# A hybrid decoder step on one core: warm-up products over ones, unscaled value sums, squares added on VectorE, and another order of the output chunks

## The chip, the cores and the metric

The kernel runs as one program on one core of a Trainium2 chip. The metric is the device time of one execution in microseconds (us); lower is better. The engines are PE (matrix products; PEld is its weight load), DVE (VectorE), ACT (ScalarE), POOL (GpSimd) and SP, whose queue issues nearly all transfers.

## The reference, cut to what matters

Two layers are applied to a prompt of 512 tokens and to 32 sample tokens (8 sequences of 4) with a page cache of 2,048 positions. All values are float32.

```python
def _layer(x, ...):
    h = _rmsnorm(x, norm_w)
    z = h @ w_in                                     # 1024 -> 3584 columns
    rq, rk, rv, rg, mq, mk, mv, mg, pu, pg = split(z)
    r_o, S_new = _retention(rope(rq), rope(rk) / 8, rv, S0, gn_w)
    m_o = moba_attend(rope(rmsnorm(mq)), rope(rmsnorm(mk)), mv)
    p_o, buf_new = _pool_mixer(pu, pool_buf, ...)
    mix = concat(r_o * silu(rg), m_o * silu(mg), p_o * silu(pg))
    return x + mix @ w_out, S_new, mk, mv, buf_new   # x twice: prompt, sample
```

The RMS norm is `x * rsqrt(mean(x*x) + eps) * norm_w`. Since a token's `rsqrt` is one number, a projection may be taken of `x * norm_w` and scaled by it afterwards; layer 0 of the kernel does that.

## The kernel before, in words

**Products.** Each dense product is split in two parts per operand: `whl` holds a weight slice's high part (a rounded copy by ACT) and its low part (the difference, by DVE or POOL), `XT` the same of the tokens, features on partitions. A product is three passes (`PASSES`, L475): high by high, low tokens by high weights, high tokens by low weights. The weights come in chunks of four slices of 256 features each: `mv`, `mq`, `mk`, `pu`, `pg`, `mg`, `rq`, `rv`, `rk`, `rg`, then the output projection `o0`, `o1` (384 columns) and `o2` (256 columns). A token tile (128 tokens) of a 384-column chunk is 24 products of 128x384, of `o2` 24 of 128x256.

**Order.** `_Plan` (L119) lays out all engines ahead of time while the program is built: each task asks for an engine (`R`), names flags that it needs and buffers that it takes, and the earliest task by planned times is written next. Each engine then runs its instructions in that fixed order and waits only on semaphores. Dense products have the lowest rank and fill the gaps; attention over cached pages (`dec`, `pv`), transposes (`tr`) and prompt attention (`att`) go ahead of them. Five `whl` buffers hold one chunk's four slices and the next chunk's first. A changed duration, rank or flag can move instructions everywhere.

**Start.** `start` (L1640) loads the first tokens on ACT's queue; `load_weights` and `load_tokens` take the rest in turn on SP's. Tokens lie in two halves `h` of 256 and four feature pairs `kp`: `split_tokens` makes `XT` from `mix`, scaled by `ncol` (the norm's weights). `norm_tokens` squares the tokens into `qT` (half 0) and `kT` (half 1), adds over features, and a product with `ones` (`tr<-ones,qT`) sums over partitions. PE's first real work is `mv`, half 0 in the `acc` sums, half 1 in `att`. One product of zeros (`warm`) stands ahead of it.

**Between the layers.** `post_out` adds the residual to a tile of the output projection; with the last chunk the tile is whole and `rmsnorm` of layer 1 can run: ACT squares, POOL takes the root, DVE multiplies, PE transposes (`tr<-cst,qT` for tiles 0 and 1, `kT` for 2 and 3, `PT` for the sample), ACT and DVE write `XT`.

Of the kernel before, what the change touches and what calls it, by code (L numbers as in the profile page):

```python
# [111 lines left out]


SP_PRIO = 2
WARM = 1


class _Plan:
# [198 lines left out]
def trunk(ctx, tc, depth, xp, xt, xs, xst, kv, sret, spool, pt, nrow, ncol, lpar, w384, w256, cst, y0,  # L317
# [108 lines left out]
        G.tensor_tensor(out=out, in0=out, in1=mhalf[:rows, :n], op=OP.pow)  # L426


    order = ["mv", "mq", "mk", "pu", "pg", "mg", "rq", "rv", "rk", "rg", "o0", "o1", "o2"]
    chunks = [(l, n) for l in range(depth) for n in order]  # L430
    wt, raws, readers = {}, {}, {}

# [28 lines left out]
    def split_weights():  # L461
        for ci, (l, n) in enumerate(chunks):
            W2 = 2 * width(n)
            for s_ in slices(n):
                yield R("ACT", [("raw", ci, s_)], ["whl"])
                hl = wt[ci, s_] = buf("whl")
                A.copy(hl[:, 0, :W2], raws[ci, s_][:, :W2])

                def low(hl=hl, W2=W2, ci=ci, s_=s_):
                    yield R("DVE|POOL")  # L470
                    add2(hl[:, 1, :W2], raws[ci, s_][:, :W2], hl[:, 0, :W2].bitcast(F32), OP.subtract)
                    read_raw(ci, s_)
                    X.flag("w", ci, s_)

                X.spawn(low(), 2, X.then())  # L475
# [2 lines left out]
    KS_IN = list(range(8))  # L478
    KS_OUT = [6, 7, 4, 5, 2, 3, 0, 1]

    def tok_piece(ci, n, t, a, ks, i):

        W = width(n)
        k = ks[i]
        w0, w1 = (wt[ci, k // 2][:, lo, (k % 2) * W:(k % 2 + 1) * W] for lo in range(2))
        for j, (xl, wl) in enumerate(PASSES):
            mm(a[:, :W], XT[:, k, xl, t * 128:(t + 1) * 128], w1 if wl else w0,
               start=i == 0 and j == 0, stop=i == 7 and j == 2)

    def feat_piece(ci, n, f, half, a, ks, i):  # L490
# [318 lines left out]
    def layer(l):  # L809
# [702 lines left out]

        def residual():

            for name in ("o0", "o1", "o2"):
# [12 lines left out]
        def post_out(name, t):  # L1528
# [4 lines left out]
            def f(a):  # L1533
                if t < 4:
                    yield R("DVE", got)
                    res = L["res", name, t]
                    out = ytile(t, c0, W)
                    V.tensor_tensor(out=out, in0=col3(a[:, :W]), in1=col3(res[:, :W]), op=OP.add)
                    X.put("acc")
                else:  # L1540
                    yield R("DVE", (), ["t1"])
                    z_ = buf("t1")[:NS, :W]
                    yield from join_sample(a, z_, W)
                    yield R("DVE", got)
                    res = L["res", name, t]
                    V.tensor_tensor(out=z_, in0=z_, in1=res[:NS, :W], op=OP.add)
                X.put("qk")
                if t == 4:
                    yield R("SP")
                    S.dma_start(o_ys[:, c0:c0 + W] if l == depth - 1 else y0[SEQ:, c0:c0 + W], z_)  # L1550
                    at = X.dma(48)
                    X.put("t1", at=at)
                    if name == "o2":
                        X.flag("ys", l + 1, at=at)
                elif l == depth - 1:
                    send(col3(o_yp[t * 128:t * 128 + 128, c0:c0 + W]), out, W / 2)
                elif name == "o2":
                    X.flag("y", l + 1, t)
                    send(col3(y0[t * 128:t * 128 + rows, :]), ytile(t), 512)
            return f  # L1560

        def dense():
# [18 lines left out]
            else:  # L1581

                for h in range(2):
                    for kp in range(4):
                        yield R("PE", [("w", ci, kp), ("xk", h, kp)], [] if kp else ["att" if h else "acc"] * 2)
                        if kp == 0:
                            a = [ps("acc") for _ in range(2)] if h == 0 else [ps("att")] * 2
                            a = a if h == 0 else [x[:, j] for j, x in enumerate(a)]
                        for j in range(2):
                            for k in (2 * kp, 2 * kp + 1):  # L1590
                                tok_piece(ci, "mv", 2 * h + j, a[j], KS_IN, k)
                        if h:
                            X.put("whl")
                    for j in range(2):
# [44 lines left out]

    def start():  # L1640
        yield R("ACT")
        nc.scalar.dma_start(mix[:, 0:2, 0:256], col3_(xt[0, 0]))
        X.use("ACT", 0.06)
        X.flag("xt", 0, 0, at=X.now + 3.0)
        yield R("SP")
        S.dma_start(ncolt, ncol)
        X.flag("ncol", at=X.dma(4))
        X.spawn(load_weights(), 3)
        X.spawn(split_weights(), 4)
        X.spawn(load_tokens(), 2)  # L1650
# [2 lines left out]
        for h in range(2):  # L1653
            for kp in range(4):
                X.spawn(split_tokens(h, kp), 1)
            X.spawn(norm_tokens(h), 2)
        X.spawn(split_sample(), 1)
        layers[0]["begin"]()

# [27 lines left out]
    def split_tokens(h, kp):  # L1687

        cs = slice(256 * h, 256 * h + 256)
        ks = (2 * kp, 2 * kp + 1)  # L1690
        yield R("ACT|DVE", [("xt", h, kp), ("ncol",)])
        for k in ks:
            if X.engine == "ACT":
                A.activation(XT[:, k, 0, cs], mix[:, k, cs], AF.Copy, scale=ncolt[:, k:k + 1])
            else:
                V.tensor_scalar(XT[:, k, 0, cs], mix[:, k, cs], ncolt[:, k:k + 1], None, op0=OP.mult)
        yield R("DVE")
        for k in ks:
            V.scalar_tensor_tensor(XT[:, k, 1, cs], mix[:, k, cs], ncolt[:, k:k + 1], XT[:, k, 0, cs].bitcast(F32),
# [3 lines left out]
    def norm_tokens(h):  # L1703

        cs = slice(256 * h, 256 * h + 256)
        tag = ("qT", "kT")[h]
        for i in range(2):
            yield R("ACT|POOL", [("xt", h, 2 * i), ("xt", h, 2 * i + 1)], [] if i else [tag])
            if i == 0:
                sq = buf(tag)[:, :2048].rearrange("p (k n) -> p k n", k=8)  # L1710
            x = mix[:, 4 * i:4 * i + 4, cs]
            if X.engine == "ACT":
                A.activation(sq[:, 4 * i:4 * i + 4], x, AF.Square)
            else:
                G.tensor_tensor(out=sq[:, 4 * i:4 * i + 4], in0=x, in1=x, op=OP.mult)
        yield R("DVE|POOL")
        add2(sq[:, 0:4], sq[:, 0:4], sq[:, 4:8], OP.add)
        yield R("DVE|POOL")
        add2(sq[:, 0:2], sq[:, 0:2], sq[:, 2:4], OP.add)
        yield R("DVE|POOL")  # L1720
        add2(sq[:, 0], sq[:, 0], sq[:, 1], OP.add)
        yield R("PE", [("zeros",)], ["tr"])
        p = ps("tr")
        for j in range(2):
# [60 lines left out]

    def clear():
        yield R("POOL")
        G.memset(qblk, 0.0)
        G.memset(ones, 1.0)
        X.flag("zeros")  # L1790
        G.memset(mhalf, -0.5)
        for s_ in Sst:
# [3 lines left out]

    def warm(n):

        yield R("PE", [("zeros",)], ["att", "att"])
        o_ = ps("att")[:, 0]  # L1800
        for _ in range(n):
            mm(o_[:, :384], qblk[:, 0, 0:4, :].rearrange("p b r -> p (b r)"),
               qblk[:, 0:2].rearrange("p i b r -> p (i b r)")[:, :384])
        X.put("att", 2)

    layers = [layer(l) for l in range(depth)]
# [3 lines left out]
            yield from layers[l]["dense"]()  # L1810

    X.spawn(start(), 0)
    X.spawn(warm(1), 0)
    X.spawn(clear(), 0)
    X.spawn(dense(), 9)
    X.run()
# [84 lines left out]
```

## Time and profile before

| | us |
|---|---|
| median of 3 runs | 698.95 (697.78 to 700.24) |
| profiled execution | 699.1 |
| its span | 697.3 |
| PE busy | 679.0 (97%) |
| DVE, ACT, POOL busy | 486.5, 334.0, 104.3 |

The profile has one execution. Its span is the time from the first to the last recorded work; the profiled time is 1.8 us longer. A busy PE is not PE at its peak: matmuls are pipelined, and the recorded ends are modelled.

### The profile page before, as it was taken

To read this page: it belongs to the slowest core of one execution; us is meant where nothing else is said; L and a number is where in the kernel's file an instruction comes from. 1 tells how busy PE (TensorE), PEld (TensorE's weight loads), DVE (VectorE), ACT (ScalarE), POOL (GpSimd) and SP (SyncE) were. 2 spreads that over 40 slices of the span, in tenths; PEclk is the share of its full clock that TensorE was granted. 3 is DMA by queue.
4 is the path that set the end of the run, shared out by engine and by line. 5 is a ranking of instruction groups with operands and counts; after the bars stand their busy time and mean duration, and the time that the engine had idled before them with its cause. 6 is when DMAs were issued, how large, how long until landed. Compare 5 with 4: busy or idle time off the path is not lost.

```text
span 697.3 us, 16968 instructions
## 1 busy us (share of the span) xinstructions
PE 679.0 (97%) x5940; PEld 570.0 (82%) x5940; DVE 486.5 (70%) x1155; ACT 334.0 (48%) x847; POOL 104.3 (15%) x132
## 2 busy tenths in 40 slices
PE   7999999999999999999999999999999999999998
PEld 6997767777877887899988778777687878989998
DVE  6889888677663569975494699775846455897642
ACT  7553676652342333364363437676723324256520
POOL 4332223000000012300021223230100000051000
PEclk9999999999999999999999999999999999999999
DMA  9667899699979964335553887999988997020552
GB/s 320 226 214 238 271 317 320 209 293 299 306 246 335 320 243 148 100 127 181 188 174 126 271 256 256 301 320 288 295 281 284 316 308 250 4 96 5 169 181 79
DMA packets 111366, 159.76 MB, mean 229 GB/s; under 512 B 13937, under 2 KB 96114, under 8 KB 111282
## 3 DMA queue, kind: packets, MB, share of 16 engines
q1 hardware_dynamic: 111010, 158.43, 69.8%
q8 instruction: 47, 0.77, 0.4%
q10 hardware_dynamic: 272, 0.26, 0.2%
q14 instruction: 37, 0.30, 0.1%
HBM read 148.80 MB, written 9.84 MB: 228 GB/s over the span
## 4 chain that ended last, share of the span: by engine, by line
PE 79%; DVE 12%; DMA 4%; issue 2%; ACT 2%; POOL 1%; DVEq 0%; ACTq 0%
PE acc L349 50%; PE pv L349 10%; PE dec L349 10%; PE tr L359 5%; PE att L349 4%; DVE whl L311 2%; DMA wraw<-w 2%; DVE qk L311 1%; DVE t L311 1%; DMA pk<-kv 1%; DVE acc L311 1%; DVE qT L311 1%; DMA mix<-xt 1%; DVE P L311 1%; DVE qst L311 1%
## 5 line engine op out<-in xcount | busy, mean ns | idle before, releaser
L349 PE MATMUL acc<-whl,XT 128*128 128x384 f32 (+1 forms) x1680 | 309.9, 337 | 4.1 <-ACT whl L311 3.2
L349 PEld LDWEIGHTS acc<-whl,XT 128*128 128x128 f32 x1680 | 281.3, 189 | 23.5 <-issue 14.5
L349 PE MATMUL acc<-XT,whl 128*128 128x256 f32 (+1 forms) x960 | 136.6, 294 | 0.9 <-ACT pt L311 0.5
L349 PEld LDWEIGHTS acc<-XT,whl 128*128 128x128 f32 x960 | 124.0, 189 | 9.6 <-issue 6.4
L311 ACT CAST whl<-wraw 128x768 fp32r<-128x768 f32 (+1 forms) x100 | 76.8, 782 | 47.2 <-PE acc L349 37.7
L311 DVE TENSOR_TENSOR whl<-wraw,whl 128x768 fp32r<-128x768 f32 (+1 forms) x92 | 85.4, 941 | 18.1 <-ACT whl L311 17.0
L349 PE MATMUL dec<-pk,qblk 128*32 128x256 f32 x768 | 49.5, 383 | 0.7 <-issue 0.6
L349 PEld LDWEIGHTS dec<-pk,qblk 128*32 128x32 f32 x768 | 23.0, 109 | 18.5 <-issue 4.9
L311 DVE TENSOR_TENSOR pv<-pv,cst 128x384 f32<-128x384 f32 x40 | 22.5, 561 | 21.3 <-PE pv L349 21.0
L311 ACT ACTIVATE P<-att,ast 128x128 f32<-128x128 f32 (+3 forms) x48 | 25.3, 531 | 10.6 <-DVE ast L311 10.0
L311 DVE TENSOR_TENSOR mix<-acc,qk 128x384 f32<-128x384 f32 (+1 forms) x24 | 12.2, 508 | 24.8 <-PE acc L349 24.6
L311 POOL TENSOR_TENSOR qst<-qst,mhalf 128x6 f32<-128x6 f32 (+1 forms) x20 | 26.5, 1323 | 1.7
L311 ACT ACTIVATE t<-acc 128x256 f32<-128x256 f32 (+1 forms) x32 | 12.6, 392 | 23.6 <-DVE acc L311 14.0
L311 ACT ACTIVATE dP<-dec,stat 128x256 f32<-128x256 f32 x32 | 15.1, 472 | 17.7 <-DVE stat L311 17.5
L311 ACT ACTIVATE dPT<-dec 128x256 f32<-128x256 f32 x32 | 12.2, 381 | 21.0 <-PE pv L349 20.9
L311 ACT COPY PT<-tr 128x384 f32<-128x384 f32 (+3 forms) x42 | 16.8, 433 | 11.1 <-PE tr L359 10.9
L311 POOL TENSOR_SCALAR gst<-gst 128x6 f32<-128x6 f32 (+1 forms) x12 | 3.7, 306 | 120.4 <-DVE gst L311 108.3
L311 POOL TENSOR_TENSOR gst<-gst,reps 128x6 f32<-128x6 f32 x4 | 0.9, 219 | 138.3 <-DVE gst L311 138.3
L311 POOL TENSOR_TENSOR whl<-wraw,whl 128x768 fp32r<-128x768 f32 (+1 forms) x8 | 15.4, 1922 | 38.9 <-issue 28.5
L311 DVE TENSOR_REDUCE stat<-dec 128x1 f32<-128x256 f32 x32 | 13.5, 421 | 11.0 <-PE dec L349 10.7
L311 ACT ACTIVATE PT<-PT,gst 128x64 f32<-128x64 f32 x48 | 16.8, 428 | 8.6 <-POOL gst L311 8.6
L349 PE MATMUL pv<-PT,tv 128*64 128x128 f32 x240 | 19.3, 283 | 1.2 <-ACT PT L311 1.1
(503 smaller groups left out, 1202.9 us busy)
## 6 DMA issues: line engine op xcount, KB each, us to landing
pk<-kv SPq DMA_DIRECT2D x256, 192.0 KB, 3.7
wraw<-w SPq DMA_DIRECT2D x76, 384.0 KB, 5.0
wraw<-w SPq DMA_DIRECT2D x24, 256.0 KB, 4.1
y<-mix SPq DMA_DIRECT2D x4, 512.0 KB, 3.6
mix<-xt SPq DMA_DIRECT2D x7, 256.0 KB, 6.0
pk<-w SPq DMA_DIRECT2D x4, 384.0 KB, 5.1
o_vp<-tv SPq DMA_DIRECT2D x8, 192.0 KB, 2.3
o_kp<-qk SPq DMA_DIRECT2D x8, 192.0 KB, 4.5
```

What stands on the lines that cost most here:

```text
L311: return f(*args, **kw)
L349: nc.tensor.matmul(out, lhsT, rhs, start=start, stop=stop)
L359: nc.tensor.transpose(out, in_, ident[:n, :n])
```

## The change

- `OUTS`: weights and products of the output projection go in the order `o0`, `o2`, `o1`; what was tied to the last chunk `o2` is tied to `o1`.
- `warm`: ten products of 128x128 over `ones` stand in place of one of 128x384 over the zeros of `qblk`; POOL writes `ones` first.
- `start`: the first token block comes in two transfers, and `ncol` between them, all on ACT's queue; `ncol` leaves SP's queue.
- The first weight slice is rounded in two halves, the first tokens are split by DVE, and half 0 of `mv` runs pass by pass, each pass with a flag of its own (`wh`, `xh`: the high part is there).
- `norm_tokens`: ACT squares in three pieces (features 0 to 2, 3 to 5, 6 and 7 of eight), and DVE alone adds, in five additions in place of three that DVE or POOL took; the rank is 5 in place of 2.
- `post_mv`: the sums of `mv` are copied out of PSUM as they are, and in layer 0 scaled in place afterwards.

```diff
+OUTS = ["o0", "o2", "o1"]
-WARM = 1
+WARM = 10
+NORM = 5
...
-                A.copy(hl[:, 0, :W2], raws[ci, s_][:, :W2])
+                for c0, c1 in ((0, W2 // 2), (W2 // 2, W2)) if ci + s_ == 0 else ((0, W2),):
+                    A.copy(hl[:, 0, c0:c1], raws[ci, s_][:, c0:c1])
+                X.flag("wh", ci, s_)
...
-                    yield from scaled_copy(lambda: L["tv"][:, t], a[:, :384], t, [("tvb", l)])
+                    yield R("ACT|DVE", [("tvb", l)])
+                    copy(L["tv"][:, t], a[:, :384])
                     X.put("acc" if l or t < 2 else "att")
+                    if l == 0:
+                        yield from scaled_copy(lambda: L["tv"][:, t], L["tv"][:, t], t)
...
-                        yield R("PE", [("w", ci, kp), ("xk", h, kp)], [] if kp else ["att" if h else "acc"] * 2)
...
+                        for ps_ in range(3) if h == 0 else (None,):
+                            key = [("w", ci, kp), ("xk", h, kp)] if h else [(("wh", "wh", "w")[ps_], ci, kp),
+                                                                           (("xh", "xk", "xk")[ps_], h, kp)]
+                            yield R("PE", key, [] if kp or ps_ else ["att" if h else "acc"] * 2)
...
-            for n in ("o0", "o1", "o2"):
+            for n in OUTS:
                 yield from tokens(n, lambda t: post_out(n, t), lambda t: [("mix", l, t)], KS_OUT)
...
-        nc.scalar.dma_start(mix[:, 0:2, 0:256], col3_(xt[0, 0]))
+        for f in range(2):
+            nc.scalar.dma_start(mix[:, f, 0:256], xt[0, 0][:, 256 * f:256 * f + 256])
+            if f == 0:
+                nc.scalar.dma_start(ncolt, ncol)
...
-        yield R("SP")
-        S.dma_start(ncolt, ncol)
...
-        yield R("ACT|DVE", [("xt", h, kp), ("ncol",)])
+        yield R("ACT|DVE" if h + kp else "DVE", [("xt", h, kp), ("ncol",)])
...
-        for i in range(2):
-            yield R("ACT|POOL", [("xt", h, 2 * i), ("xt", h, 2 * i + 1)], [] if i else [tag])
...
+        for k0, k1 in ((0, 3), (3, 6), (6, 8)):
+            yield R("ACT", [("xt", h, k // 2) for k in range(k0, k1)], [] if k0 else [tag])
...
+            A.activation(sq[:, k0:k1], mix[:, k0:k1, cs], AF.Square)
+            if k0 == 3:
+                yield R("DVE")
+                add2(sq[:, 0:3], sq[:, 0:3], sq[:, 3:6], OP.add)
+                for k in (1, 2):
+                    yield R("DVE")
+                    add2(sq[:, 0], sq[:, 0], sq[:, k], OP.add)
+        for k in (6, 7):
+            yield R("DVE")
+            add2(sq[:, 0], sq[:, 0], sq[:, k], OP.add)
...
+        G.memset(ones, 1.0)
+        X.flag("ones")
...
-            mm(o_[:, :384], qblk[:, 0, 0:4, :].rearrange("p b r -> p (b r)"),
-               qblk[:, 0:2].rearrange("p i b r -> p (i b r)")[:, :384])
+            mm(o_[:, :128], ones, ones)
```

PE's first instructions before (`att<-whl` is half 1 of `mv`, `tr<-ones` are the sums of squares, `dec<-pk,X_71` is the sample's part of `mv`, `dec<-wraw` of `mq`; the later `acc` are `mq`):

```order
L349 MATMUL att<-qblk 128x384
L349 MATMUL acc<-whl,XT 128x384 x48
L349 MATMUL att<-whl,XT 128x384 x36
L349 MATMUL tr<-ones,ssum 32x1 x4
L349 MATMUL att<-whl,XT 128x384 x12
L349 MATMUL tr<-ones,qT 128x1 x2
L349 MATMUL dec<-pk,X_71 32x192 x16
L349 MATMUL tr<-ones,kT 128x1 x2
L349 MATMUL acc<-whl,XT 128x384 x12
```

And now:

```order
L351 MATMUL att<-ones 128x128 x10
L351 MATMUL acc<-whl,XT 128x384 x48
L351 MATMUL att<-whl,XT 128x384 x24
L351 MATMUL tr<-ones,ssum 32x1 x4
L351 MATMUL att<-whl,XT 128x384 x12
L351 MATMUL dec<-pk,X_71 32x192 x16
L351 MATMUL att<-whl,XT 128x384 x12
L351 MATMUL acc<-whl,XT 128x384 x6
L351 MATMUL dec<-wraw,X_71 32x192 x16
L351 MATMUL acc<-whl,XT 128x384 x6
L351 MATMUL tr<-ones,qT 128x1 x2
```

Ten short products stand first, and the sum of squares of half 0 moved behind twelve products of `mq` and both samples.

DVE's instructions around the sums of squares before, from the sample's sums (`ssum`) on:

```order
L311 TENSOR_REDUCE ssum<-Rb 128x32
L311 TENSOR_TENSOR qT<-qT 128x512
L311 TENSOR_TENSOR kT<-kT 128x1024
L311 TENSOR_SCALAR rs<-tr 128x1
L311 TENSOR_TENSOR qT<-qT 128x256
L311 TENSOR_TENSOR kT<-kT 128x512
```

And now:

```order
L313 COPY tv<-acc 128x384
L313 TENSOR_SCALAR rs<-tr 128x1
L313 TENSOR_TENSOR whl<-wraw,whl 128x768 x2
L313 TENSOR_TENSOR qT<-qT 128x768
L313 TENSOR_TENSOR whl<-wraw,whl 128x768 x2
L313 SCALAR_TENSOR_TENSOR ks<-dec,rs,t_353 32x192 x2
L313 TENSOR_TENSOR qT<-qT 128x256 x2
L313 TENSOR_TENSOR kT<-kT 128x768
L313 TENSOR_TENSOR vst<-ks,vst 32x384
L313 TENSOR_TENSOR kT<-kT 128x256 x2
L313 TENSOR_TENSOR qT<-qT 128x256 x2
```

The four low parts of `mq`'s weights now stand ahead of most of the additions, and the last two for half 0 at the end.

PE between the layers before, from the middle of `o2` (128x256) on (`tr<-cst` are transposes of normalized tokens; the 128x384 products are `mv` of layer 1):

```order
L349 MATMUL acc<-whl,XT 128x256 x24
L359 MATMUL tr<-cst,qT 128x128 x4
L349 MATMUL acc<-whl,XT 128x256 x6
L359 MATMUL tr<-cst,qT 128x128 x4
L349 MATMUL acc<-whl,XT 128x384 x6
L359 MATMUL tr<-cst,PT 128x32 x8
L359 MATMUL tr<-cst,kT 128x128 x8
L349 MATMUL dec<-wraw,X_71 32x192 x16
L349 MATMUL acc<-whl,XT 128x384 x6
L359 MATMUL tr<-cst,kT 128x128 x8
```

And now (the 128x384 products are `o1` up to the `PT` transposes, and `mv` behind them):

```order
L351 MATMUL acc<-whl,XT 128x384 x54
L361 MATMUL tr<-cst,qT 128x128 x8
L351 MATMUL acc<-whl,XT 128x384 x18
L361 MATMUL tr<-cst,qT 128x128 x4
L351 MATMUL acc<-whl,XT 128x384 x6
L361 MATMUL tr<-cst,qT 128x128 x4
L351 MATMUL acc<-whl,XT 128x384 x18
L361 MATMUL tr<-cst,PT 128x32 x8
L351 MATMUL acc<-whl,XT 128x384 x12
L361 MATMUL tr<-cst,kT 128x128 x4
L351 MATMUL acc<-whl,XT 128x384 x6
L361 MATMUL tr<-cst,kT 128x128 x4
```

Behind each tile's last product more products now stand before the transposes that need that tile.

## Rows read from the trace of the kernel before

**Rows 1.** The page's busy line and its chain, shares by engine.

```profile
PE 679.0 (97%) x5940; PEld 570.0 (82%) x5940; DVE 486.5 (70%) x1155; ACT 334.0 (48%) x847; POOL 104.3 (15%) x132
...
PE 79%; DVE 12%; DMA 4%; issue 2%; ACT 2%; POOL 1%; DVEq 0%; ACTq 0%
```

**Rows 2.** Stretches of 20 us: busy by engine, granted PE clock, DMA share, GB/s.

```profile
20.00:40.00 20.00, 19.90 (x171) 18.15 (x170) 17.09 (x38) 9.04 (x20) 8.91 (x11) 1.00 0.72 232
...
680.00:697.30 17.30, 14.11 (x112) 13.91 (x110) 4.57 (x9) 1.44 (x3) 0.00 (x0) 0.97 0.27 80
```

**Rows 3.** Timeline of the first 17 us: start, us, engine, instruction, idle before.

```profile
0.73 0.41 SPq L1646 DMA_DIRECT2D ncol<-ncol  x1
1.19 0.90 SPq L456 DMA_DIRECT2D pk<-w  x2
...
1.52 1.65 PE L349 MATMUL att<-qblk 128*128 128x384 f32 x2 [1.52 <-POOL qblk L311]
...
4.71 0.91 ACT L311 ACTIVATE XT<-mix,ncol 128x256 fp32r<-128x256 f32 x2 [1.02 <-DMA mix<-xt]
...
5.53 1.55 ACT L311 CAST whl<-pk 128x768 fp32r<-128x768 f32 x2
...
6.37 1.83 DVE L311 TENSOR_TENSOR whl<-pk,whl 128x768 fp32r<-128x768 f32 x2 [0.23 <-ACT whl L311]
...
12.96 0.88 DVE L311 SCALAR_TENSOR_TENSOR XT<-mix,ncol,XT 128x256 fp32r<-128x256 f32 x2
...
13.50 2.61 POOL L311 TENSOR_TENSOR qT<-qT 128x1024 f32<-128x1024 f32 x1 [8.28 <-ACT qT L311]
13.75 2.77 DVE L311 TENSOR_SCALAR XT<-mix,ncol 128x256 fp32r<-128x256 f32 x2
...
16.83 6.57 PE L349 MATMUL att<-whl,XT 128*128 128x384 f32 x36
```

**Rows 4.** PE alone in two stretches of the start: busy, products, granted clock.

```profile
6.39:10.20 3.81, 3.81 (x11) 1.00 1.05 384
10.20:16.80 6.60, 6.60 (x39) 1.00 1.07 374
```

**Rows 5.** Weight transfers of the first chunk: least, median, greatest time to landing.

```profile
DMA to landing us min/median/max: 4.0/5.1/6.1
```

**Rows 6.** Timeline between the layers (PE's pieces, and tile 0's square and norm).

```profile
342.23 1.06 ACT L311 ACTIVATE qT<-mix 128x1024 f32<-128x1024 f32 x1 [2.48 <-DVE mix L311]
...
344.35 1.41 DVE L311 SCALAR_TENSOR_TENSOR qT<-mix,rst,pt 128x512 f32<-128x512 f32 x2 [2.16 <-POOL rst L311]
...
345.69 0.46 PEld L359 LDWEIGHTS tr<-cst,qT 128*128 128x128 f32 x4
...
351.63 1.30 PE L349 MATMUL acc<-whl,XT 128*128 128x384 f32 x6
353.89 0.43 PE L359 MATMUL tr<-cst,PT 32*128 32x32 f32 x4 [0.50 <-DVE XT L311]
355.51 1.97 PE L359 MATMUL tr<-cst,kT 128*128 128x128 f32 x8 [1.19 <-DVE XT L311]
...
360.44 1.03 PE L359 MATMUL tr<-cst,kT 128*128 128x128 f32 x8
361.23 0.95 PE L349 MATMUL acc<-whl,XT 128*128 128x384 f32 x4
```

**Rows 7.** Stretch between the layers in which the granted clock fell.

```profile
354.90:358.30 3.40, 2.79 (x20) 2.16 (x24) 3.37 (x5) 1.72 (x6) 3.30 (x3) 0.50 0.39 117
```

**Rows 8.** The end: two of VectorE's last additions; stores by size, us to landing.

```profile
683.28 0.54 DVE L311 TENSOR_TENSOR mix<-acc,qk 128x384 f32<-128x384 f32 x1
...
694.15 0.43 DVE L311 TENSOR_TENSOR mix<-acc,qk 128x256 f32<-128x256 f32 x1 [2.42 <-PE acc L349]
...
o_yp<-mix SPq DMA_DIRECT2D x4, 128.0 KB, 1.9
...
o_yp<-mix SPq DMA_DIRECT2D x1, 192.0 KB, 2.6
```

More of the change, by code (lines that the diff above doesn't have):

```diff
@@ L426, in rsq @@
         G.tensor_tensor(out=out, in0=out, in1=mhalf[:rows, :n], op=OP.pow)
-    order = ["mv", "mq", "mk", "pu", "pg", "mg", "rq", "rv", "rk", "rg", "o0", "o1", "o2"]
+    order = ["mv", "mq", "mk", "pu", "pg", "mg", "rq", "rv", "rk", "rg"] + OUTS
     chunks = [(l, n) for l in range(depth) for n in order]
@@ L479, in trunk, with tok_piece @@
     KS_OUT = [6, 7, 4, 5, 2, 3, 0, 1]
-    def tok_piece(ci, n, t, a, ks, i):
+    def tok_piece(ci, n, t, a, ks, i, one=None):
         W = width(n)
         k = ks[i]
-        w0, w1 = (wt[ci, k // 2][:, lo, (k % 2) * W:(k % 2 + 1) * W] for lo in range(2))
         for j, (xl, wl) in enumerate(PASSES):
-            mm(a[:, :W], XT[:, k, xl, t * 128:(t + 1) * 128], w1 if wl else w0,
+            if one not in (None, j):
+                continue
+            mm(a[:, :W], XT[:, k, xl, t * 128:(t + 1) * 128], wt[ci, k // 2][:, wl, (k % 2) * W:(k % 2 + 1) * W],
                start=i == 0 and j == 0, stop=i == 7 and j == 2)
@@ L1513, in residual @@
         def residual():
-            for name in ("o0", "o1", "o2"):
+            for name in OUTS:
                 c0, W = OUTC[name]
@@ L1552, in f @@
                     X.put("t1", at=at)
-                    if name == "o2":
+                    if name == OUTS[-1]:
                         X.flag("ys", l + 1, at=at)
@@ L1556, in f @@
                     send(col3(o_yp[t * 128:t * 128 + 128, c0:c0 + W]), out, W / 2)
-                elif name == "o2":
+                elif name == OUTS[-1]:
                     X.flag("y", l + 1, t)
@@ L1584, in dense @@
                     for kp in range(4):
-                        yield R("PE", [("w", ci, kp), ("xk", h, kp)], [] if kp else ["att" if h else "acc"] * 2)
[L1586 to L1589, printed above, removed]
+                        for ps_ in range(3) if h == 0 else (None,):
+                            key = [("w", ci, kp), ("xk", h, kp)] if h else [(("wh", "wh", "w")[ps_], ci, kp),
+                                                                           (("xh", "xk", "xk")[ps_], h, kp)]
+                            yield R("PE", key, [] if kp or ps_ else ["att" if h else "acc"] * 2)
+                            if kp == 0 and not ps_:
+                                a = [ps("acc") for _ in range(2)] if h == 0 else [ps("att")] * 2
+                                a = a if h == 0 else [x[:, j] for j, x in enumerate(a)]
                             for k in (2 * kp, 2 * kp + 1):
-                                tok_piece(ci, "mv", 2 * h + j, a[j], KS_IN, k)
+                                for j in range(2):
+                                    tok_piece(ci, "mv", 2 * h + j, a[j], KS_IN, k, ps_)
                         if h:
@@ L1641, in start @@
         yield R("ACT")
-        nc.scalar.dma_start(mix[:, 0:2, 0:256], col3_(xt[0, 0]))
-        X.use("ACT", 0.06)
+        for f in range(2):
+            nc.scalar.dma_start(mix[:, f, 0:256], xt[0, 0][:, 256 * f:256 * f + 256])
+            if f == 0:
+                nc.scalar.dma_start(ncolt, ncol)
+        X.use("ACT", 0.18)
         X.flag("xt", 0, 0, at=X.now + 3.0)
-        yield R("SP")
-        S.dma_start(ncolt, ncol)
-        X.flag("ncol", at=X.dma(4))
+        X.flag("ncol", at=X.now + 2.9)
         X.spawn(load_weights(), 3)
@@ L1655, in start @@
                 X.spawn(split_tokens(h, kp), 1)
-            X.spawn(norm_tokens(h), 2)
+            X.spawn(norm_tokens(h), NORM)
         X.spawn(split_sample(), 1)
@@ L1696, in split_tokens @@
                 V.tensor_scalar(XT[:, k, 0, cs], mix[:, k, cs], ncolt[:, k:k + 1], None, op0=OP.mult)
+        X.flag("xh", h, kp)
         yield R("DVE")
@@ L1706, in norm_tokens @@
         tag = ("qT", "kT")[h]
-        for i in range(2):
-            yield R("ACT|POOL", [("xt", h, 2 * i), ("xt", h, 2 * i + 1)], [] if i else [tag])
-            if i == 0:
+        for k0, k1 in ((0, 3), (3, 6), (6, 8)):
+            yield R("ACT", [("xt", h, k // 2) for k in range(k0, k1)], [] if k0 else [tag])
+            if k0 == 0:
                 sq = buf(tag)[:, :2048].rearrange("p (k n) -> p k n", k=8)
[L1711 to L1721, printed above, removed]
+            A.activation(sq[:, k0:k1], mix[:, k0:k1, cs], AF.Square)
[8 more added lines that the diff above has]
+            add2(sq[:, 0], sq[:, 0], sq[:, k], OP.add)
         yield R("PE", [("zeros",)], ["tr"])
@@ L1787, in clear @@
         yield R("POOL")
+        G.memset(ones, 1.0)
+        X.flag("ones")
+        yield R("POOL")
         G.memset(qblk, 0.0)
-        G.memset(ones, 1.0)
         X.flag("zeros")
@@ L1797, in warm @@
     def warm(n):
-        yield R("PE", [("zeros",)], ["att", "att"])
+        yield R("PE", [("ones",)], ["att", "att"])
         o_ = ps("att")[:, 0]
         for _ in range(n):
-            mm(o_[:, :384], qblk[:, 0, 0:4, :].rearrange("p b r -> p (b r)"),
-               qblk[:, 0:2].rearrange("p i b r -> p (i b r)")[:, :384])
+            mm(o_[:, :128], ones, ones)
+            X.use("PE", 0.2)
         X.put("att", 2)
@@ L1812, in trunk @@
     X.spawn(start(), 0)
-    X.spawn(warm(1), 0)
+    X.spawn(warm(WARM), 0)
     X.spawn(clear(), 0)
```

## The prediction

> **What bounds the kernel now.** I read the busy line of the page and the chain first, then stretches of 20 us, then the timeline wherever PE is idle. PE is busy for 679.0 of 697.3 us and holds 79% of the chain [rows 1], and the change takes no dense product away. So it can only win or lose where PE waits or runs slowly, and what the reader is to look for is the 18.3 us of idle (697.3 - 679.0) and where they lie. The start has 4.7 us of them: the first `mv` product comes at 6.39, and before it only the 1.65 us of the zero product are busy [rows 3, 4]. The end has 3.2 us (17.30 - 14.11 [rows 2]). Between the layers two waits make 1.7 us (0.50 + 1.19 [rows 6]). The other 8.7 us are spread thinly over the two layers.
>
> Two stretches cost more than their idle time. From 6.39 to 10.20 PE does 11 products in 3.81 us, 0.35 us each; right behind it 39 in 6.60 us, 0.17 us each [rows 4]. The granted clock reads 1.00 in both, but the spacing halves within one form of product, as between the levels of 1.2 and 2.4 GHz; PE had stood idle for 3.2 us before the first and was busy before the second. Between the layers the clock row itself shows the lower level, 0.50 from 354.90 to 358.30 [rows 7], behind those two waits.
>
> The profiled execution took 699.1 us, its span 697.3 and 1.8 around it; the median of the runs is 698.95, 0.15 lower. I sum against 699.1 and take 0.15 off.
>
> **Start.** Added: ten products of 128x128 over `ones`, free for PE as nothing else can run there. The old one of 384 columns took 1.65 us [rows 3], so ten of a third of the columns take between 1.65 / 3 x 10 = 5.5 us and less if fixed parts of that one are not repeated; they end near 6 us at the latest, when `mv` would begin, and PE enters `mv` busy. The 11 slow products would then take 11 x 0.17 = 1.9 us and not 3.81.
>
> But PE then runs into its data. I walk the queues. SP loses the issue of `ncol` and sends the first weights at 0.73 in place of 1.19 [rows 3]; with 4.0 us to landing [rows 5] they are there at 4.7. ACT need not split tokens first (0.91 us at 4.71 [rows 3]); half a slice is half of some 0.8 us of cast (two slices took 1.55), so the first high-by-high product can start at about 5.2 in place of 6.39. The whole slice is cast at 5.6, its low part on DVE is done about 1.0 later (two took 1.83 [rows 3]), and the first pair's last pass ends near 7.4. From there ACT and DVE set the pace: for pair 2 ACT's square stands ahead of the cast of the third slice, as it does now (1024 columns take 1.06 us in the row of the same operation [rows 6], so 0.8 for 768), and DVE does in a row a low part (0.95), two token splits, two token lows (0.88), the sample's product (some 0.4) and the fourth low part (0.95). The two token splits took 2.77 us while POOL added `qT` [rows 3]; as POOL does not square or add any more, I take 0.6 us, with 2.77 as the other end. That puts the last low part at about 14.1 and the end of half 0 at about 14.8, against 16.83 now, when half 1 begins: -2.0 us. The ends: if PE never waited, 48 products at 0.17 from 5.2 would end at 13.4, -3.4 us; if the transfers hold everything where it is, 0.
>
> Half 1 keeps its pace (6.57 us for 36 products [rows 3]), since its low parts need 0.44 us per feature (0.88 for two) and PE takes 1.04. Behind it PE comes to `tr<-ones,qT`, at about 29 us by adding up its queue. DVE has by then to do four low parts of `mq` (3.8 us), the sample's values (the nearest row of that size is a token low of 0.44 each) and the additions (768 columns like a low part of 768, 0.95; 256 like a token low, 0.44). From the end of the token lows near 18 us this puts the last addition at 29 to 30. I charge 0.3 us of wait for it. What queues behind this wait is all of PE, the next 36 products of `mq` first. Start in sum: -1.7 us.
>
> The copies of the value sums out of PSUM are one pass as before; the four scalings are added, on ACT, which has half of its time free (48% [rows 1]): nothing. If ACT were late there, a projected tile would wait by one such pass, some 0.5 us, inside the bounds of the middle.
>
> **Between the layers.** With `o1` last, each tile's products before the transposes that need it are longer. Now tile 0's square starts at 342.23 and its transposes at 345.69 [rows 6]: with some 0.1 for the hop, 3.6 us behind the addition. In the new order 30 wide products (54 less the 24 of tile 0), 5.2 us, stand between the end of tile 0 and its transposes; for tile 3 it is the `PT` transposes (two of 0.43 [rows 6]), 18 products (3.1), tile 2's transposes (0.8) and the sample's `mv` (from the end of the first `kT` group at 357.48 to 360.44 lie 3.0 us with it and six wide products, which take 1.3; so at most 1.7 [rows 6]), 4.8 to 6.5 us; I take 6, since a part of that ran at the lower clock. DVE's queue behind tile 3's addition (0.54 [rows 8]) is three low parts of weights (2.85), two short token lows and the norm (1.41 [rows 6]), 5.4 us: just in time. So I take both waits (1.69 us) as gone, and with them the fall of the clock. That fall costs at least the difference of the two like groups of transposes: the first `kT` group is busy for 1.97 us, the second for 1.03, 0.9 us. At most it costs half of its 3.4 us, 1.7. So 2.6 to 3.4 us go; I take 2.8, nearer to what the rows show. The other end: a DVE that is late by as much as now leaves all of it, 0.
>
> **End.** The last addition is wide: 0.54 in place of 0.43 [rows 8], +0.1. The last store has 192 KB: the one such row needs 2.6 us, those of 128 KB 1.9, so +0.7, though the 192 KB store had other traffic beside it. I take +0.5 for both, ends 0.1 and 0.8.
>
> **The middle.** Since the planner lays everything out again, some five hundred switches between kinds of products stand elsewhere. Nothing in the trace says whether the 8.7 us of thin idle grow or shrink. POOL gives three low parts of weights to DVE (POOL's column of the order has three fewer), 2.9 us on an engine that is busy 17.09 of 20 us behind the start [rows 2]; against that DVE is not held up by POOL any more (2.77 against 0.6). I take 0, with a third of the thin idle, 2.9 us, either way.
>
> **Sum.** -1.7 - 2.8 + 0.5 = -4.0: 699.1 - 4.0 - 0.15 = 695.0 us.
>
> **Rivals.**
> First, the transfers hold the start. For: the DMA queues moved 384 and 374 GB/s from 6.39 to 16.80 with a busy share over 1.0 [rows 4], and the last of the first weights took 6.1 us to land [rows 5]; against: PE had no idle time from 6.39 on, so data did not hold the slow products. The start then brings 0, and 699.1 - 2.8 + 0.5 - 0.15 = 696.65. The Trainium skill, "DMA: Bandwidth & Descriptors", section "Issuing engines are not separate DMA queues", speaks for this rival: transfers issued by different engines end up on the same 16 DMA engines and interleave, so moving `ncol` and tokens to ACT's queue buys no bandwidth. By that rule alone the start would stay where it is; the trace agrees as far as the full share goes, and no run here shows the split transfer.
>
> Second, the pause between the layers stays: DVE, 5.4 us of queue against 6, is late by a little, the clock falls, and only the start is won: 699.1 - 1.7 + 0.5 - 0.15 = 697.75.
>
> Third, slower. DVE's additions come so late that PE stops at `tr<-ones,qT`. For: they stand behind four low parts and behind what ACT squares last, on an engine that is nearly full. Each us of lateness is one of PE, and if the stop is as long as the waits between the layers (1.7 us) the clock falls too, another 1.7 at most. It decides once DVE is more than 4.4 us late: 4.4 + 1.7 makes 6.1, which eats the 4.0 and the 2.1 of the bound below. At 5 us late: 695.0 + 5 + 1.7 = 701.7. Against: by my sum it is late by 1 us at most.
>
> Fourth, the middle wins as well: 695.0 - 2.9 = 692.1.
>
> **How the numbers follow.** Chances: forecast 0.54, transfers hold the start 0.18, pause stays 0.12, slower 0.08, middle wins 0.08. A measurement of this kernel can tell some 0.3% from no change, 2.1 us: faster is below 696.85, slower above 701.05. Faster are nearly all of the forecast (0.50), over half of the first rival (0.10), a little of the second (0.02) and the fourth (0.08): 0.70. Slower is the third, 0.08; the rest, 0.22, is no change. The forecast's own range is 695.0 with 2.9 below (the middle) and 2.0 above, 692 to 697. The range reaches to the second rival: 691.8 to 698.2.
>
> **What would show it.** Right: the spacing of the first `mv` products is 0.17 us from the start, half 1 (`att`) begins near 15 us, no wait and no granted clock of 0.50 near 350 us, and PE's idle time falls by some 3 us. Wrong: products of 0.35 us again behind the warm ones; half 1 at 16.5 or later; PE idle ahead of `tr<-ones,qT`; a `tr<-cst,kT` that waits for DVE; or new idle time of 2 us and more in one of the stretches between 40 and 340 or 360 and 680 us.

## The result and the profile after

The changed kernel takes 690.82 us (median of 6 runs, 690.34 to 692.05), the kernel before in the same comparison 699.14 us; the ratio is 0.9892 (95% interval 0.9878 to 0.9907). That is 8.3 us faster, where the forecast was 4.0 us and the range ended at 691.8. The profiled execution took 690.34 us, its span 688.6 against 697.3.

The page's busy line and its chain, in the columns of [rows 1]:

```profile
PE 674.9 (98%) x5958; PEld 570.9 (83%) x5958; DVE 490.4 (71%) x1181; ACT 329.8 (48%) x835; POOL 96.9 (14%) x129
...
PE 79%; DVE 13%; POOL 2%; issue 2%; DMA 2%; ACT 2%; ACTq 0%; DVEq 0%; SPq 0%; POOLq 0%
```

PE's idle time fell from 18.3 to 13.7 us (688.6 - 674.9), and its busy time by 4.1 us (679.0 - 674.9), though ten products over `ones` were added. To see where, I divide both timelines at three products: the first of layer 0's output projection, the first of layer 1's `mq`, and the last dense product (counted along the products that read `whl`).

| stretch, us | before | after | difference | forecast |
|---|---|---|---|---|
| start and layer 0, to its output projection | 299.03 | 297.31 | -1.72 | start -1.7, middle 0 |
| pause: from there to layer 1's `mq` | 78.66 | 75.17 | -3.49 | -2.8 |
| layer 1: from there to the last dense product | 316.14 | 312.05 | -4.09 | middle 0 |
| end: from there to the end of the span | 3.47 | 4.07 | +0.60 | +0.5 |

Three of the four lines are near their forecast. The gain that was not forecast lies in layer 1, which the change touches directly only in the order of its output projection. Each stretch is read from one execution; the six of after lie within 1.7 us, and the profiled one is the fastest of them.

Timeline of after: the start (six rows), four rows in layer 0 around a new wait, the pause, and the last addition.

```profile
0.99 4.63 PE L351 MATMUL att<-ones 128*128 128x128 f32 x20 [0.99 <-POOL ones L313]
...
5.52 2.31 PE L351 MATMUL acc<-whl,XT 128*128 128x384 f32 x8
...
8.00 7.27 PE L351 MATMUL acc<-whl,XT 128*128 128x384 f32 x40 [0.18 <-DVE whl L313]
...
11.19 0.61 DVE L313 TENSOR_SCALAR XT<-mix,ncol 128x256 fp32r<-128x256 f32 x2
...
15.11 2.10 PE L351 MATMUL att<-whl,XT 128*128 128x384 f32 x11
...
29.28 0.50 PE L351 MATMUL tr<-ones,qT 128*128 128x1 f32 x4
...
49.90 1.99 POOL L313 TENSOR_TENSOR whl<-wraw,whl 128x768 fp32r<-128x768 f32 x1 [1.12 <-ACT whl L313]
...
50.12 2.59 DVE L313 TENSOR_TENSOR whl<-wraw,whl 128x768 fp32r<-128x768 f32 x1
...
57.86 0.90 PE L361 MATMUL tr<-cst,qk 128*128 128x128 f32 x3 [2.40 <-DVE qk L313]
58.41 4.68 PE L351 MATMUL acc<-whl,XT 128*128 128x384 f32 x18
...
349.89 0.68 PE L361 MATMUL tr<-cst,PT 32*128 32x32 f32 x8
350.50 2.37 PE L351 MATMUL acc<-whl,XT 128*128 128x384 f32 x12
352.71 0.60 PE L361 MATMUL tr<-cst,kT 128*128 128x128 f32 x4
...
356.17 1.15 PE L361 MATMUL tr<-cst,kT 128*128 128x128 f32 x8
...
684.90 0.56 DVE L313 TENSOR_TENSOR mix<-acc,qk 128x384 f32<-128x384 f32 x1 [3.66 <-PE acc L351]
```

Read against [rows 3, 6, 8]: the products over `ones` keep PE busy until the first `mv` product at 5.52 (the next two still come 0.45 and 0.47 us apart, at 5.97 and 6.44; from 6.79 on the spacing is 0.17 us), the two token splits take 0.61 us where they took 2.77 beside POOL, half 1 begins at 15.11 and not 16.83, PE does not wait at `tr<-ones,qT`, and the transposes between the layers start without a wait. New is the wait of 2.40 us at 57.86: POOL and DVE do a low part at the same time, DVE's takes 2.59 us, and PE waits for DVE.

Stretches of after: the pause, the place behind the new wait, the part of layer 1 in which the idle time differs most, and the whole of layer 1 as in the table (columns as in [rows 2]).

```profile
340.00:360.00 20.00, 20.00 (x154) 18.80 (x153) 16.47 (x30) 14.24 (x30) 4.49 (x9) 1.00 0.47 142
...
58.00:60.00 2.00, 2.00 (x8) 2.00 (x9) 1.24 (x4) 1.17 (x3) 0.00 (x0) 0.50 0.86 267
...
380.00:600.00 220.00, 219.98 (x2026) 176.34 (x2026) 158.14 (x374) 103.89 (x282) 25.34 (x28) 1.00 0.85 272
...
372.48:684.53 312.05, 310.45 (x2777) 260.08 (x2776) 217.23 (x531) 141.86 (x373) 39.81 (x51) 1.00 0.71 225
```

The same of before:

```profile
340.00:360.00 20.00, 18.29 (x161) 16.62 (x160) 15.29 (x26) 11.93 (x26) 6.60 (x12) 0.91 0.56 168
...
380.00:600.00 220.00, 216.65 (x1970) 170.29 (x1970) 150.43 (x344) 106.22 (x296) 28.66 (x28) 1.00 0.85 276
...
377.69:693.83 316.14, 312.76 (x2776) 261.23 (x2776) 213.02 (x515) 146.88 (x389) 41.83 (x49) 1.00 0.69 222
```

From 380 to 600 us PE was idle for 3.35 us before (220.00 - 216.65) and is idle for 0.02 us after. DVE has more work there after than before (158 against 150 us), so it is not load that went: it stands in another order. Over the whole of layer 1 the idle time falls by less, from 3.38 to 1.60 us, since after has four waits of 0.2 to 0.5 us behind 600 us that before has not. The other 2.31 us of layer 1's 4.09 are busy time: the same products keep PE busy for 310.45 in place of 312.76 us, at a granted clock of 1.00 in both. No run here shows why.

One of before's waits there, on its timeline: DVE's low part at 403.43 meets POOL's at 402.73 and takes 1.96 us; PE runs out of products that don't need DVE and stands before `tr<-cst,qk`.

```profile
402.73 1.84 POOL L311 TENSOR_TENSOR whl<-wraw,whl 128x768 fp32r<-128x768 f32 x1 [1.93 <-ACT whl L311]
...
403.43 1.96 DVE L311 TENSOR_TENSOR whl<-wraw,whl 128x768 fp32r<-128x768 f32 x1
...
405.59 3.43 PE L349 MATMUL acc<-whl,XT 128*128 128x384 f32 x18
409.82 0.55 PE L359 MATMUL tr<-cst,qk 128*128 128x128 f32 x3 [0.81 <-DVE qk L311]
```

Three more waits follow, at 435.70 (0.71 us, behind DVE), 438.63 (0.46, behind ACT) and 499.64 (1.07, behind ACT, which had itself waited for DVE at 498.33). After has none of the four.

### The profile page after: what moved, and what is told of

It reads as the page before. It is cut to its first block, busy times and chain, and to the rows that moved or that the text cites. A ratio compares the mean times of both kernels' runs of the same rounds, so it can differ in the third digit from the quotient of the medians.

```text
span 688.6 us, 17002 instructions
## 1 busy us (share of the span) xinstructions
PE 674.9 (98%) x5958; PEld 570.9 (83%) x5958; DVE 490.4 (71%) x1181; ACT 329.8 (48%) x835; POOL 96.9 (14%) x129
## 4 chain that ended last, share of the span: by engine, by line
PE 79%; DVE 13%; POOL 2%; issue 2%; DMA 2%; ACT 2%; ACTq 0%; DVEq 0%; SPq 0%; POOLq 0%
PE acc L351 50%; PE dec L351 10%; PE pv L351 10%; PE tr L361 6%; PE att L351 4%; DVE whl L313 2%; DVE qk L313 1%; POOL gst L313 1%; DVE t L313 1%; POOL qst L313 1%; DVE qT L313 1%; ACT PT L313 1%; DVE bns L313 1%; DMA qk<-y 1%; DVE row L313 1%
## 5 line engine op out<-in xcount | busy, mean ns | idle before, releaser
L351 PE MATMUL acc<-XT,whl 128*128 128x256 f32 (+1 forms) x960 | 138.0, 295 | 1.7 <-DVE qk L313 1.2
L313 DVE TENSOR_TENSOR whl<-wraw,whl 128x768 fp32r<-128x768 f32 (+1 forms) x96 | 87.3, 920 | 13.9 <-ACT whl L313 13.1
L351 PE MATMUL dec<-pk,qblk 128*32 128x256 f32 x768 | 48.1, 383 | 0.0
L361 PE MATMUL tr<-cst,qk 128*128 128x128 f32 (+1 forms) x108 | 18.4, 280 | 4.7 <-DVE qk L313 4.6
L361 PEld LDWEIGHTS tr<-cst,qk 128*128 128x128 f32 (+1 forms) x108 | 12.3, 142 | 11.2 <-DVE qk L313 4.7
L313 DVE TENSOR_TENSOR t<-acc,cst 128x192 f32<-128x192 f32 x32 | 9.9, 351 | 16.1 <-PE acc L351 16.1
L313 DVE TENSOR_REDUCE ast<-att 128x2 f32<-128x256 f32 (+3 forms) x24 | 19.8, 825 | 0.8
```

The source lines that it names most:

```text
L313: return f(*args, **kw)
L351: nc.tensor.matmul(out, lhsT, rhs, start=start, stop=stop)
L361: nc.tensor.transpose(out, in_, ident[:n, :n])
```

## The experiments

Theories on layer 1. **P**: POOL's low parts stretch DVE's work, and PE waits. **O**: `o1` in place of `o2` at the end is what layer 1's gain hangs on. **S**: the new start alone brings it. **R**: layer 1's waits belong to the order that the planner happens to lay out; a new layout has other waits, and this one was lucky.

**The change taken apart.** The changed kernel with the old order of the output projection:

```diff
-OUTS = ["o0", "o2", "o1"]
+OUTS = ["o0", "o1", "o2"]
```

> The changed kernel with the old order of the output chunks (o0, o1, o2), so the start alone is changed. Theory P (the part of the gain that the prediction did not have comes from POOL: a weight's low part on POOL stretches DVE's additions, and PE waits): the start brings 1.7 us, the pause between the layers stays, and the middle goes by how many low parts stand on POOL (7 here, 8 before, 4 in the changed kernel): 697 us, about 0.997 of before. Theory O (the new order of the output chunks brings layer 1's gain by itself, since layer 1 starts without a backlog on DVE): 697 to 698 us too, but layer 1 as before. Theory S (the start alone brings more than 1.7): 694 us or less.

Measured: 698.14 us, ratio 0.9989 (0.9974 to 1.0004): by the median the start alone can't be told from no change. The kernel before with the new order alone (its literals `"o0", "o1", "o2"` replaced by the list):

```diff
+OUTS = ["o0", "o2", "o1"]
-            for name in ("o0", "o1", "o2"):
+            for name in OUTS:
```

> The kernel before with the order o0, o2, o1 of the output chunks and nothing else. Theory P: the pause goes (3.3 us) and the store at the end costs 0.5; five low parts are on POOL in place of eight, so 1 to 3 us more may go: 693.5 to 696 us. Theory O: 3.3 + 4.1 - 0.5 = 6.9 us less, 692.2 us. Theory S: 696.3 us.

Measured: 692.72 us, ratio 0.9919 (0.9893 to 0.9945). So the new order brings most of it: the pause takes 75.53 us and layer 1 312.31. With the old order layer 1 takes 316.40, and the pause has its two waits still and a third behind them, as its timeline shows. The granted clock does not fall there, and yet the pause is no shorter than before's (78.99 and 78.66 us):

```profile
352.67 0.43 PE L361 MATMUL tr<-cst,PT 32*128 32x32 f32 x4 [0.50 <-DVE XT L313]
354.28 1.09 PE L361 MATMUL tr<-cst,kT 128*128 128x128 f32 x8 [1.18 <-DVE XT L313]
...
358.97 1.25 PE L361 MATMUL tr<-cst,kT 128*128 128x128 f32 x8 [0.90 <-DVE XT L313]
...
340.00:360.00 20.00, 17.38 (x161) 15.68 (x159) 15.39 (x25) 11.84 (x26) 6.61 (x12) 1.00 0.63 196
```

S falls. These two runs can't tell O from R, since layer 1's order of PE is before's in the first and after's in the second.

**POOL's low parts.** All low parts on DVE, in before and in after:

```diff
-                    yield R("DVE|POOL")
+                    yield R("DVE")
```

> The kernel before with all low parts of weights on DVE, none on POOL; nothing else is edited, the plan lays the order out anew. Theory P: the waits of PE behind POOL's low parts (at 88, 409, 435, 438 and 498 us, some 5 us in all) go, one low part of DVE costs 0.95 us on an engine with room: 694 to 696 us. Rival R (layer 1's gain is the chance of a newly laid-out order): 699 us, 2 either way.

> The changed kernel with all low parts of weights on DVE. Theory P: POOL's low part at 49.9 us stretches one on DVE from 0.95 to 2.59 us, PE waits 2.4 us at 55.5 and then runs for 3.4 us at half its clock; without it 3 to 4 us go, and 0.5 to 1 at 266 and 602: 686.5 to 688 us. Rival R: 691 us, 2 either way.

Measured: 699.03 us, ratio 1.0003 (0.9986 to 1.0020), and 693.0 us, ratio 0.9924 (0.9895 to 0.9953). Both fit R and miss P. The stretched pairs go, but DVE is late elsewhere. In the first, PE waits at 280 us, where it had no such wait:

```profile
279.90 0.30 PE L359 MATMUL tr<-cst,row 128*64 128x128 f32 x1 [1.02 <-DVE row L311]
282.57 1.95 PE L349 MATMUL acc<-XT,whl 128*128 128x256 f32 x12 [2.37 <-DVE t L311]
284.32 0.41 PE L359 MATMUL tr<-cst,row 128*64 128x128 f32 x1
284.39 4.51 PE L349 MATMUL acc<-XT,whl 128*128 128x256 f32 x24
```

Then only at the places of the waits: in after for layer 0's first three chunks, in before for layer 1's `mv` to `rq`.

```diff
-                    yield R("DVE|POOL")
+                    yield R("DVE" if ci <= 2 else "DVE|POOL")        # after
+                    yield R("DVE" if 12 < ci <= 19 else "DVE|POOL")  # before
```

> The changed kernel, only that the low parts of layer 0's first three weight chunks are all done by VectorE; GpSimd keeps three of its four low parts. Theory P-local (a GpSimd low part beside VectorE's work stretches VectorE's additions, and TensorE then waits): the 2.40 us wait at 57.9 us and the 3.4 us of half clock behind it go, nothing new comes, 690.8 - 2.6 to 4 = 687 to 688 us. Rival (VectorE is too full at the start to take a fourth low part: the work is late by as much): a wait of 1 us and more between 28 and 60 us, 690 to 691.5 us. Rival R (any new order of the rest moves by chance): 689 to 694 us with new waits behind 60 us.

> The kernel before, only that the low parts of layer 1's chunks mv to rq, three of which GpSimd does, are all done by VectorE; the other low parts stay where they are allowed to be. Theory P-local: the four waits at 409, 435, 438 and 498 us go (1.15 + 1.0 + 0.74 + 1.35 = 4.2 us) and no wait of the same size stands in their place, 695 us. Rival: VectorE is full and the work is late in another place (as when all low parts were taken from GpSimd: 699.0 us), 698 to 700 us with waits of 1 us and more somewhere from 360 to 690 us.

Measured: 688.97 us, ratio 0.9859 (0.9828 to 0.9890), and 701.61 us, ratio 1.0044 (1.0027 to 1.0062). In the first, PE's order is that of after in both layers, and the price of the pair can be read: DVE's low part takes 0.95 us where it took 2.59, PE's wait there is 0.75 us where it was 2.40, and the clock does not fall.

```profile
50.44 0.95 DVE L313 TENSOR_TENSOR whl<-wraw,whl 128x768 fp32r<-128x768 f32 x1
...
58.00:60.00 2.00, 2.00 (x14) 2.00 (x13) 1.70 (x5) 1.40 (x6) 0.00 (x0) 1.00 0.75 227
```

Layer 0's output projection begins at 295.56, 1.75 us earlier than in after, and the median is the lowest of all kernels here; its interval touches that of after (0.9878 to 0.9907), so that it beats after is likely and not settled. P-local had 687 to 688: layer 1 took 1.02 us longer than in after (313.07), in the same order of PE. In the second the four waits were to go and 4 us with them (on PE's own rows above they make 3.05). Layer 1's order changed throughout, and a wait about as long as the four together stands behind them; in the 30 us around it (610 to 640) the granted clock is 0.89:

```profile
616.83 0.42 PE L359 MATMUL tr<-cst,row 128*64 128x128 f32 x1 [2.92 <-DVE row L311]
```

Layer 1 takes 319.99 us. P is right about the waits that it named and wrong about the sum.

**The warm products.** One product over `ones` and not ten, all other instructions in after's order:

```diff
-        for _ in range(n):
-            mm(o_[:, :128], ones, ones)
+        for i in range(n):
+            if i == 0:
+                mm(o_[:, :128], ones, ones)
+            else:
+                X.array(FULL, 2 * (128 / 1200 + 0.003))
```

> The changed kernel with one product over ones at its start in place of ten; all other instructions in the same order. Theory W (the warm products are what takes the slow products away): the first mv products stand 0.35 us apart again, some 12 of them; a part is hidden behind ACT's and VectorE's splitting of weights, so half 1 begins 0 to 1.5 us later and the time is 690.8 + 0.3 to 1.5 = 691.1 to 692.3 us. Rival D (the data set the pace of the start; the clock does nothing there): half 1 begins within 0.2 us of where it does now, 690.8 us.

Measured: 692.47 us, ratio 0.9903 (0.9866 to 0.9940), which can't be told from after. The timeline can: half 0 takes 10.54 us in one piece, and half 1 begins 0.79 us later than in after.

```profile
5.51 10.54 PE L351 MATMUL acc<-whl,XT 128*128 128x384 f32 x48 [3.73 <-ACT whl L313]
15.90 2.27 PE L351 MATMUL att<-whl,XT 128*128 128x384 f32 x12
...
58.64 0.55 PE L361 MATMUL tr<-cst,qk 128*128 128x128 f32 x3 [2.39 <-DVE qk L313]
58.94 3.41 PE L351 MATMUL acc<-whl,XT 128*128 128x384 f32 x18
```

So the warm products are worth 0.5 to 0.8 us of the start: in the kernels with ten of them half 1 begins at 15.04 to 15.45, here at 15.90. That the rest of the start's gain comes from data that is there earlier was not tested by itself. The second pair of rows is the same wait as in after (2.39 and 2.40 us), here without the fall of the clock: 18 products take 3.41 us where after's took 4.68.

**Another layout.** The planner is told that one operation of layer 1's norm takes 0.3, 0.6 or 1.0 us longer than it thought. That moves rows of the order and gives some operations to another engine (in before with 1.0, eight net go from ACT to DVE); PE's instructions stay the same. `d` is the number in the run's text:

```diff
+            X.use("ACT", d)
```

> The kernel before with only the planned time of one ACT operation, the square in layer 1's norm, 0.3 us longer: no instruction is changed, the planner lays layer 1 out anew. Theory R (what layer 1 takes is set by chance each time it is laid out): from layer 1's first mv product on it takes another 2 to 4 us more or less than before's 316.1 us up to the last product, 695 to 702 us. Theory O (it is o1 at the end that brings layer 1's gain): within 1.5 us of 316.1, 697.5 to 700.5 us.

> The kernel before with the planned time of the square in layer 1's norm 0.6 us longer, no instruction changed: another order of layer 1. By theory R (each order has waits of its own, what they sum to is chance) layer 1 takes from its first mq product to the last dense product anything from 312 to 320 us, where before takes 316.1 and the nudge of 0.3 us took 313.4. By theory O (o2 at the end costs layer 1 its 4 us) it stays above 314.

> The kernel before with the planned time of the square in layer 1's norm 1.0 us longer, no instruction changed. Theory R: from layer 1's first mq product to the last dense product 312 to 320 us; theory O: above 314 us. The pause between the layers (from layer 0's output projection to layer 1's first mq product, 78.7 us in before) stays above 78 us by both.

> The changed kernel with the planned time of the square in layer 1's norm 0.3 us longer, no instruction changed. Theory R: from layer 1's first mq product to the last dense product it takes not 312.0 us as now but 313 to 318, and the time is 691 to 697 us. Theory O: within 1 us of 312, 690 to 692 us. By both the pause stays short: 75.2 us from layer 0's output projection to layer 1's first mq product, give or take 0.7.

> The changed kernel with the planned time of the square in layer 1's norm 1.0 us longer, no instruction changed. Theory R: from layer 1's first mq product to the last dense product 313 to 318 us, 691 to 697 us in all. Theory O: within 1 us of 312, 690 to 692 us. The pause by both 75.2 us, give or take 0.7.

Measured, in the order of the texts: 699.0, 700.48 and 698.4 us for before, ratios 1.0004 (0.9987 to 1.0020), 1.0036 (1.0012 to 1.0061), 1.0002 (0.9987 to 1.0017); 695.43 and 694.1 us for after, ratios 0.9937 (0.9908 to 0.9965) and 0.9950 (0.9919 to 0.9981). By PE's order of layer 1 (two kernels share one where PE's rows stand in the same sequence there):

| PE's order of layer 1 | kernels | last chunk | pause, us | layer 1, us | both, us |
|---|---|---|---|---|---|
| before's | before; old output order | `o2` | 78.66; 78.99 | 316.14; 316.40 | 394.80; 395.39 |
| before's | after + 1.0 | `o1` | 75.49 | 315.17 | 390.66 |
| after's | after; new output order alone; one warm product; three chunks on DVE | `o1` | 75.17; 75.53; 75.54; 75.16 | 312.05; 312.31; 314.07; 313.07 | 387.22; 387.84; 389.61; 388.23 |
| a third | before + 0.3; before + 1.0 | `o2` | 83.21; 82.50 | 313.35; 311.78 | 396.56; 394.28 |
| a fourth | before + 0.6 | `o2` | 80.64 | 315.37 | 396.01 |
| a fifth | after + 0.3 | `o1` | 75.39 | 316.61 | 392.00 |

Each entry is one execution: kernels of one order differ by up to 2.0 us in layer 1 (312.05 and 314.07), so smaller differences between orders say nothing. The profiled execution of after + 1.0, 691.81 us, is its fastest, 2.3 us below its median.

The changed kernel with 1.0 us more is the sharpest of them: from the 31st product of layer 1's `mv` into the output projection its PE instructions, 2,580 of them, stand exactly as before's do. Before's waits come back with them. From its timeline and its stretches:

```profile
395.86 1.84 POOL L313 TENSOR_TENSOR whl<-wraw,whl 128x768 fp32r<-128x768 f32 x1 [1.93 <-ACT whl L313]
...
396.55 1.96 DVE L313 TENSOR_TENSOR whl<-wraw,whl 128x768 fp32r<-128x768 f32 x1
...
402.95 0.55 PE L361 MATMUL tr<-cst,qk 128*128 128x128 f32 x3 [0.80 <-DVE qk L313]
...
492.71 1.09 PE L351 MATMUL pv<-PT,tv 128*64 128x128 f32 x14 [1.06 <-ACT PT L313]
...
380.00:600.00 220.00, 216.96 (x1980) 171.08 (x1979) 153.64 (x354) 105.07 (x289) 29.23 (x29) 1.00 0.84 268
```

PE is idle there for 3.04 us, before for 3.35. O falls twice for layer 1 alone: with `o1` last layer 1 can take 316.61, and with `o2` last 311.78 (where R had 312 at least). P as the whole cause falls too: the fifth order has no low part on POOL from 380 to 600 us and is idle for 3.77 us, as its stretch shows (220.00 - 216.23); it waits for other work of DVE, longest on its timeline before `pv<-vst,oPT`.

```profile
459.12 0.41 PE L351 MATMUL pv<-vst,oPT 96*128 96x384 f32 x1 [2.14 <-DVE oPT L313]
...
380.00:600.00 220.00, 216.23 (x1990) 172.63 (x1990) 157.15 (x362) 100.11 (x274) 24.36 (x27) 1.00 0.82 266
```

R holds for layer 1 by itself. And O's other half, the pause, is robust: all orders with `o1` last take 75.2 to 75.5 us in it, all with `o2` last 78.7 to 83.2 (the kernels with moved low parts left out). The long pauses go with the short layers 1: with `o2` last the two add up to 394.3 to 396.6 us in all five kernels. A likely reason, not tested by itself, is that DVE catches up while PE stands.

The last column keeps something of O alive. With `o1` last the two stretches add up to 387.2 to 392.0 us in all six kernels of the table, each below all with `o2` last. Averaged over three orders of layer 1 on either side they make 390.3 and 395.5. So some 5.2 us of the 7.6 that after gains here (394.80 - 387.22) go with the new order of the chunks, whatever the layout, and the draw gives the rest: after lies 3.1 us below its mean, before 0.7 below its own. These are estimates from few layouts.

## Why the prediction was wrong

**The step that failed** is the middle: "I take 0, with a third of the thin idle, 2.9 us, either way". Layer 1 gave 4.09 us, beyond that bound. The thin idle was not thin: in before 3.35 us of the 8.7 lie from 380 to 600 us, 3.05 of them in four waits, two behind DVE and two behind ACT, that one layout has and another has not; a list of PE's longest waits with their times would have shown them. And idle time is not all that a layout moves: of the 4.09 us 1.78 are idle time and 2.31 busy time of PE with the same products, for which the forecast had no term. What makes PE busy for less stays open. The rival "middle wins as well" (692.1) was the right case and had 0.08; the measurement lies a further 1.3 us below it.

**What was luck.** Three layouts of the changed kernel with the same instructions of PE take 690.82, 694.1 and 695.43 us; the forecast of 695.0 lies between the last two, so this change was measured with its best draw of the three. Not all of the miss is luck: pause and layer 1 together were given 2.8 us, and some 5.2 of what they gained went with the new order of the chunks. The trace of before alone could not show that, since a long pause there goes with a short layer 1 in other layouts.

**Start, -1.7: right in sum.** Half 1 begins at 15.11, 1.72 us earlier (forecast 2.0, at 14.8), and `tr<-ones,qT` at 29.28 without a wait (at 29, 0.3 charged): two small misses cancel. The term for the slow products was too large: 3.81 - 1.9 was allowed for, while the first three spacings of after are still 0.45, 0.47 and 0.35 us and the warm products are worth 0.5 to 0.8.

**Layer 0 behind the start, 0: right by luck.** In the kernel with 1.0 us more, whose PE order of layer 0 is after's throughout, half 1 begins at 15.04 but the output projection at 295.33, 3.70 us earlier than in before. So layer 0's new order brought 1.9 us more there. After's execution is 1.98 us later; 1.53 of them lie between the first products of `mk` and `pu`, where its clock fell behind the wait at 57.86 and the other's did not. This wait stood in no part of the sum, and one sign of being wrong came true with it: from 40 to 340 us PE is idle for 7.15 us (300.00 - 292.85) in place of 5.15 (300.00 - 294.85), 2 us of new idle time. The forecast also counted three low parts that leave POOL; it has four fewer, four in place of eight.

**Pause, -2.8: near.** -3.49, just beyond the far end of 3.4. Both waits and the fall of the clock are gone, DVE's queue was in time, as walked. The price of the fall, 0.9 to 1.7 us of that sum, is not borne out: with the old output order the clock stayed at 1.00, a third wait of 0.90 us for DVE came, and the pause took 78.99 us all the same.

**End, +0.5: right.** The last addition stands 3.7 us before the end of the span (688.6 - 684.90) in place of 3.15 (697.3 - 694.15, [rows 8]), +0.55.

**The rivals.** Transfers do not hold the start; the pause does not stay. The slower one saw a mechanism that came, PE behind a late DVE with the clock falling, at the wrong place: it came at 57.86 and not at `tr<-ones,qT`.

## What to carry to other kernels

Where a planner writes the order, a small edit draws a new layout, and the draw alone moved this kernel's layer 1 by up to 4.6 us (312.05 to 316.61) with the same instructions of PE, where kernels of one order differ by up to 2.0: compare a change against a few layouts of either kernel before its gain is believed, and add up stretches that trade against each other, here the pause and layer 1. The waits that the trace names, summed, are a better bound for such a term than a share of the idle time, and still one that is too narrow, since busy time moves too. What a change does to one fixed place (a pause, a start, an end) could be walked through from the rows to within 0.7 us of the net, though not every part of that sum held.

## What was not expected of the hardware

Where a low part of POOL and one of DVE overlap, they do not share the time, they queue. In before POOL's ends at 404.57 (402.73 + 1.84) and DVE's at 405.39, 0.82 later, though it began at 403.43; alone it takes 0.95. In after the same: 51.89 and 52.71. So a low part given to POOL costs DVE 1.0 to 1.6 us in these two places and saves it 0.95. It need not: beside POOL's low part at 422.97 in after (1.29 us) DVE's additions read one operand from PSUM (`klz<-tr,kT`) and take no longer than elsewhere (0.56 us, against 0.54 to 0.56 over the whole trace). That taking all of them away changed nothing in before (ratio 1.0003) fits with this and does not show it, as that kernel has another order. The Trainium skill, "SBUF — State Buffer", section "SBUF: two separate sides", says it as a rule: a VectorE operation with two SBUF inputs and a GpSimd operation that reads SBUF take turns on one pair of ports, the one that comes second blocked until the first ends. The two pairs of rows agree with it.

The same wait of 2.39 or 2.40 us before `tr<-cst,qk` stands in five kernels with one order of layer 0. It was followed by 3.4 us at a granted clock of 0.50 in after, with the old output order and in after with 0.3 us more, and by none with one warm product and in after with 1.0 us more. Between the first products of `mk` and `pu` on both sides of it lie 35.35 us in each of the three and 33.82 in each of the two: the fall costs 1.5 us, and whether it comes is not settled by the wait's length alone.
